# Keeping the lo parts of w_in and w_out in DRAM, and forming the down projection's right factors in other units

## The chip, the cores and the metric

The kernel runs on one core of a Trainium2 chip. The metric is device time in microseconds (us) of one execution, as the median of several. The engines are TensorE (PE in the profile; its weight loads are listed apart as PEld), VectorE (DVE), ScalarE (ACT), GpSimd (POOL) and SyncE (SP), which here only issues DMAs; 16 DMA engines move the data.

## What is computed

One layer of a hybrid decoder for 1024 prompt tokens and 64 sample tokens (8 sequences of 8), all in float32. Cut to what matters:

```python
x = x + 0.5 * rms_norm(swiglu(rms_norm(x, g1), w_gu1, w_down1), p1)     # first FFN
z = rms_norm(x, gm) @ w_in + b_in                                       # 1024 x 2816
q, k, v, hq, hf, hi, hg = split(z)
a = windowed attention with sinks (q, k, v)
o = chunkwise gated linear recurrence (hq, hf, hi)
x = x + rms_norm(concat(norm(a), norm(o) * silu(hg)) @ w_out, pm)       # 1024 x 1024
x = x + 0.5 * rms_norm(swiglu(rms_norm(x, g2), w_gu2, w_down2), p2)     # second FFN
```

## The kernel before

**Chunks.** The tokens are cut into three chunks: chunk 0 has 256 prompt tokens and the 64 sample tokens (width 320), chunks 1 and 2 have 384 prompt tokens each (`WIDTH`, L26). Weights are read anew from DRAM for each use; SBUF does not hold them.

**Hi and lo.** A float32 matrix product is made of three products of a reduced type (`mm3`, L276: lines L278, L279 and L280). Each operand is split into hi, a rounded copy made on ScalarE, and lo, the difference, made by a subtraction on VectorE (`split`, L256: L257 and L258). `load_w` (L260) loads a weight tile of 512 KB into one of three `raw` buffers on SP's queue, takes a hi and a lo buffer from a pool (`wsp`, 8 buffers, so four tiles) and calls `split`. Chunk 0, 1 and 2 each load and split the same tiles of w_in (22 tiles: 18 column tiles by `col_tile`, four row tiles for hi) and of w_out (8 tiles).

**The mixer.** `w_in_units(n)` makes z for chunk n, `mixer(n)` the attention and the recurrence, `w_out_units(n)` the projection back. The order is at the end of `tile_step`: w_in for chunk 0, then the rest of the first FFN's down projection beside the mixer of chunk 0, then w_in for chunk 1, w_out for chunk 0, w_in for chunk 2, and so on. Mixers run as generators: each `tick()` in the code around lets them go a step further, so that their many small matmuls come to stand between the large ones. Instructions of each engine are put in order when the program is built and run in that order.

**The FFN of chunks 1 and 2.** Both chunks are computed together in each FFN by a scheme with seven products in the place of eight (Strassen's). The up projection (`up`, L847) runs over 22 units. In unit u the steps are `product(u, m)` for m = 1, 2, 6, 5, 7 in turn, and m = 4 and 3 of a unit are placed inside the next one. `evict(u, m)` takes the results out of TensorE's banks, with one multiplication on GpSimd for m = 4 and one for m = 3 (L745). The down projection needs combinations of activations (left factors) and of the weights w_down (right factors):

- `left(u)` (L768) runs when an odd unit's m = 3 is evicted: four additions on GpSimd over two units' outputs and two stores to DRAM (`FA`).
- `right_load(u)` (L780) loads four half rows of w_down on SP into two of 12 `big` buffers; `right_form(u)` (L788) makes four additions on GpSimd (L791, L792, L795, L796), in the first FFN also two splits (`in_place`), and two stores to DRAM (`FB`).

In `up`, `d` (L852) says for which odd number a right factor is loaded at a unit's m = 1 and formed at its m = 7: number 1 in unit 2, number u in unit u for the odd u from 3 on.

**The down projection** reads activations (`act`, L876, and in `begin_pair`, L936) and weights back from DRAM through `raw` and other buffers.

Of the kernel before, what the change touches and what calls it, by code (L numbers as in the profile page):

```python
# [1 line left out]

# [6 lines left out]
F32 = mybir.dt.float32  # L9
F32R = mybir.dt.float32r  # L10
# [8 lines left out]
P = 128  # L19
# [25 lines left out]
def tile_step(ctx: ExitStack, tc: tile.TileContext, A: dict, O: list):  # L45
# [224 lines left out]
    def wsrc(w, c0, n=P):  # L270
        return w[:, c0:c0 + n].rearrange("(k p) m -> p k m", p=P)
# [375 lines left out]
    def make_ffn(wgu, wdn, h, tag):  # L647
# [199 lines left out]
        def up(hooks={}):  # L847
            for i, (kind, u, m) in enumerate(f.steps):
                if kind == "p" and m == 1 and u in hooks:
                    hooks[u]()  # L850
                if kind == "p":
                    d = 1 if u == 2 else u if u % 2 and u > 1 else 0  # L852
                    if m == 1 and d:
                        right_load(d)
                    product(u, m)
                    evict(u, m)
                    if m == 7 and d:
                        right_form(d)
# [58 lines left out]
        def begin_pair(ms, inner):  # L917
            def weight(m, ks):
                n, k0 = len(ks), ks[0]
                if m in halves:  # L920
                    hi, lo = [pp.tile([P, 2, 512], F32R, tag="wsp", bufs=8, name=uid("w")) for _ in range(2)]
                    nc.sync.dma_start(hi[:, :n].bitcast(F32), FH[:, k0:k0 + n, halves[m]])
                    nc.sync.dma_start(lo[:, :n].bitcast(F32), FB[:, k0:k0 + n, {7: 0, 4: 2}[m]])
                    return hi, lo
                raw = rawslot((P, 2, 512))
                if m in (1, 2, 3):
                    r, half = (k0 if m == 1 else k0 + NK), m == 3
                    nc.sync.dma_start(raw[:, :n], wdn[r * P:(r + n) * P, half * 512:half * 512 + 512].rearrange(
                        "(k p) m -> p k m", p=P))
                else:  # L930
                    nc.sync.dma_start(raw[:, :n], FB[:, k0:k0 + n, {7: 0, 5: 1, 4: 2, 6: 3}[m]])
                hi, lo = [pp.tile([P, 2, 512], F32R, tag="wsp", bufs=8, name=uid("w")) for _ in range(2)]
                split(hi[:, :n], lo[:, :n], raw[:, :n])
                return hi, lo

            def act(m, ks):  # L936
                n, k0 = len(ks), ks[0]
                t = hslot(1).rearrange("p (k l) w -> p k l w", k=2)
                if inner:
                    raw = f.pool.tile([P, 2, 384], F32, tag="wf", bufs=4, name=uid("ar"))  # L940
                else:
# [78 lines left out]
    def mixing(tp, h):  # L1020
# [14 lines left out]
                        channel_multiplier=0)  # L1035
        G.tensor_copy(own, of)
        Z, KX, VN, MT = {}, {}, {}, {}
        state = [None]

        def bias(c):  # L1040
            return cols[:, C_BIN + c:C_BIN + c + 1]

        def col_tile(c):
            if c < 4:
                return load_w([(slice(0, 64), wsrc(w_in, 64 * c, 64)),
                               (slice(64, 128), wsrc(w_in, 256 + 64 * c, 64))], pp, "wsp", 8)
            return load_up(w_in, c * P)

        def w_in_units(n):
            w = WIDTH[n]  # L1050
# [1 line left out]
            z = Z[n] = {}  # L1052

            def tr(c, dst):
                wt = col_tile(c)
                bank = mmbank()
                proj(bank[:, :w], wt, h[n], w, range(4))
                tick()
# [458 lines left out]
        return w_in_units, mixer, w_out_units  # L1517


    def seq(*gens):  # L1520
# [70 lines left out]
                                pre_s(n, y, g, part, f2.SF, x2N[n - 1])), RB1)  # L1591

    with tc.tile_pool(name="mx", bufs=1) as tp:
        w_in_units, mixer, w_out_units = mixing(tp, hmix)
        need("c0")
        w_in_units(0)
        stream("m0", mixer(0), RM[0])
# [121 lines left out]
```

## Time and profile before

| | |
|---|---|
| Median of 3 runs | 2006.6 us (2004.51 to 2008.71) |
| Profiled execution | 2007.94 us |
| Its span, first to last instruction | 2006.2 us |
| Granted TensorE clock | 0.999 |
| Largest groups | L278, L279 and L280, all shapes: TensorE |
| Moved by DMA | 370.31 MB, 185 GB/s over the span |

Up to about 100 us the first columns of the first FFN are computed for chunk 0 alone, to about 490 its up phase runs, to about 600 the down projection of chunk 0, from about 650 to 735 w_in for chunk 0, to 855 the rest of the first FFN's down projection with the mixer of chunk 0. The mixing part of chunks 1 and 2 goes to about 1400, the second FFN to the end, its up phase from about 1435 to 1740.

A row of the profile names a line of the kernel, an engine, an operation and the tiles as out<-in, with the count, the busy time, the mean of one in ns, and the idle time before with what ended it. A wait is put down to whatever came last by semaphore. A matmul's end is modelled, so that a busy TensorE need not be at its peak; how many matmuls start in a stretch tells more.

### The profile page before, as it was taken

What the parts mean: (1) busy time and instruction counts of PE and PEld (TensorE: products, weight loads), DVE (VectorE), ACT (ScalarE), POOL (GpSimd) and SP (SyncE); (2) the same over time, 40 slices, a digit from 0 to 9 for tenths busy, and PEclk for the clock granted to TensorE, in tenths of its full rate; (3) what the DMA queues carried; (4) which work ended last, traced back from release to release, by engine and by line L of the source; (5) the groups of instructions that cost most, each with busy time, mean ns of one, the idle gap of its engine ahead of it and who ended that gap; (6) DMA issues with size and microseconds to landing.
All of it is one profiled execution on the core that took longest, in us unless ns stands there. A gap on an engine that the chain in (4) does not pass through costs nothing.

```text
span 2006.2 us, 34709 instructions
## 1 busy us (share of the span) xinstructions
PE 1983.4 (99%) x13349; PEld 1856.0 (93%) x13349; DVE 1410.5 (70%) x2303; ACT 934.5 (47%) x1689; POOL 541.5 (27%) x508
## 2 busy tenths in 40 slices
PE   9999999999999999999999999999999999999998
PEld 8999999999998987798899898988999999999886
DVE  6676667887558655777667756857888878655666
ACT  7544333444455434435344544746544444444452
POOL 0013443655104101211212311220155565510201
PEclk9999999999999999999999999999999999999999
DMA  8545446566766756766434243527566555577874
GB/s 259 169 122 179 132 129 215 202 221 226 235 217 219 190 150 215 256 166 190 135 93 144 85 143 106 175 89 235 153 198 211 184 192 192 208 231 234 285 260 138
DMA packets 377319, 370.31 MB, mean 185 GB/s; under 512 B 40546, under 2 KB 294321, under 8 KB 377137
## 3 DMA queue, kind: packets, MB, share of 16 engines
q1 hardware_dynamic: 371169, 357.21, 56.2%
q10 hardware_dynamic: 5984, 10.88, 1.6%
q8 instruction: 105, 1.72, 0.4%
q14 instruction: 61, 0.50, 0.1%
HBM read 284.31 MB, written 84.71 MB: 184 GB/s over the span
## 4 chain that ended last, share of the span: by engine, by line
PE 87%; DVE 5%; DMA 5%; ACT 2%; issue 2%; SPq 0%; DVEq 0%; ACTq 0%
PE mm L278 26%; PE mm L280 25%; PE mm L279 25%; DMA raw<-in_ffn_w_gu_dram 2%; DMA ar<-act 2%; PE pv L1196 1%; PE c L278 1%; PE c L280 1%; PE c L279 1%; PE sc L1155 1%; DVE t L707 1%; DVE w L258 1%; PE pT L1183 1%; DVE wspl L258 1%; DMA ar<-fa 1%
## 5 line engine op out<-in xcount | busy, mean ns | idle before, releaser
L278 PE MATMUL mm<-h,wsph 128*128 128x320 f32 (+1 forms) x1296 | 412.1, 320 | 2.9 <-ACT wsph L257 1.3
L280 PE MATMUL mm<-h,wspl 128*128 128x320 f32 (+1 forms) x1296 | 409.1, 317 | 1.9 <-DVE wspl L258 1.8
L279 PE MATMUL mm<-h,wsph 128*128 128x320 f32 (+1 forms) x1296 | 409.6, 317 | 0.4 <-DVE h L258 0.4
L257 ACT CAST wsph<-raw 128x1024 fp32r<-128x1024 f32 x202 | 211.4, 1049 | 280.5 <-PE mm L279 211.9
L258 DVE TENSOR_TENSOR wspl<-raw,wsph 128x1024 fp32r<-128x1024 f32 x202 | 253.1, 1257 | 123.3 <-ACT wsph L257 120.7
L258 DVE TENSOR_TENSOR w<-raw,w 128x512 fp32r<-128x512 f32 (+1 forms) x214 | 223.9, 1050 | 87.4 <-ACT w L257 86.0
L257 ACT CAST w<-raw 128x512 fp32r<-128x512 f32 (+1 forms) x214 | 158.1, 742 | 216.1 <-PE mm L279 111.7
L278 PEld LDWEIGHTS mm<-h,wsph 128*128 128x128 f32 x1296 | 242.8, 188 | 7.4 <-issue 2.5
L280 PEld LDWEIGHTS mm<-h,wspl 128*128 128x128 f32 x1296 | 243.0, 188 | 5.8 <-DVE wspl L258 2.7
L279 PEld LDWEIGHTS mm<-h,wsph 128*128 128x128 f32 x1296 | 243.3, 188 | 2.4 <-issue 1.1
L278 PE MATMUL mm<-h,w 128*128 128x384 f32 x704 | 235.4, 335 | 1.5 <-DVE big L761 1.5
L279 PE MATMUL mm<-h,w 128*128 128x384 f32 x704 | 235.6, 335 | 0.0
L280 PE MATMUL mm<-h,w 128*128 128x384 f32 x704 | 230.2, 335 | 0.0
L278 PE MATMUL mm<-w,h 128*128 128x512 f32 x462 | 181.0, 395 | 1.1 <-DVE big L956 1.1
L745 POOL TENSOR_TENSOR big<-big 128x384 f32<-128x384 f32 x88 | 113.4, 1288 | 252.5 <-ACT big L758 143.8
L279 PE MATMUL mm<-w,h 128*128 128x512 f32 x462 | 181.1, 392 | 0.0
L280 PE MATMUL mm<-w,h 128*128 128x512 f32 x462 | 179.7, 391 | 0.0
L278 PE MATMUL mm<-big,w 128*128 128x384 f32 x528 | 176.8, 335 | 1.9 <-ACT big L748 1.1
L279 PE MATMUL mm<-big,w 128*128 128x384 f32 x528 | 176.5, 334 | 0.0
L280 PE MATMUL mm<-big,w 128*128 128x384 f32 x528 | 176.4, 334 | 0.0
L258 DVE TENSOR_TENSOR w<-t,w 128x512 fp32r<-128x512 f32 x176 | 160.7, 922 | 10.7 <-ACT w L257 10.3
L278 PEld LDWEIGHTS mm<-h,w 128*128 128x128 f32 x704 | 132.1, 188 | 1.8 <-DVE big L761 1.8
(358 smaller groups left out, 3854.6 us busy)
## 6 DMA issues: line engine op xcount, KB each, us to landing
raw<-in_ffn_w_gu_dram SPq DMA_DIRECT2D x156, 512.0 KB
raw<-in_ffn_w_down_dram SPq DMA_DIRECT2D x74, 512.0 KB
raw<-in_w_in_dram SPq DMA_DIRECT2D x54, 512.0 KB
ar<-fa SPq DMA_DIRECT2D x70, 384.0 KB
big<-in_ffn_w_down_dram SPq DMA_DIRECT2D x88, 256.0 KB
fb<-big SPq DMA_DIRECT2D x44, 512.0 KB
fa<-big SPq DMA_DIRECT2D x22, 768.0 KB
raw<-fb SPq DMA_DIRECT2D x30, 512.0 KB
```

The source lines that it names most:

```text
L257: S.copy(hi, src)
L258: (lo_eng or V).tensor_tensor(lo, src, hi.bitcast(F32), op=ALU.subtract)
L278: PE.matmul(out, a[0], b[0], start=first, stop=False, skip_group_check=resume)
L279: PE.matmul(out, a[0], b[1], start=False, stop=False, skip_group_check=resume)
L280: PE.matmul(out, a[1], b[0], start=False, stop=last, skip_group_check=resume)
L707: V.tensor_tensor(t, x, y, op=ALU.subtract)
L745: G.tensor_tensor(e[:, i], e[:, i], e[:, i + 1], op=ALU.mult)
L1155: PE.matmul(banks[g][:, i * 256:i * 256 + wk], zq[64 * g:64 * g + 64, 2 * pr + i, b * P:(b + 1) * P], kx[64 * g:64 * g + 64, k0:k0 + wk], ...
L1183: PE.transpose(bank[:, (i * nk + kb) * P:(i * nk + kb + 1) * P], pt[g][:, i, kb * P:(kb + 1) * P], ident)
L1196: PE.matmul(ob[:, hd * 64:hd * 64 + 64], pT[g][:, (i * nk + kb) * P:(i * nk + kb + 1) * P], vn[:, vb, g * 64:g * 64 + 64], start=kb == 0, ...
```

## The change

1. **Lo parts.** A new function `load_lo` takes the place of `load_w` for w_in and w_out. In chunk 0 it splits as before and also stores the lo part to new DRAM tensors (LI, LV, LO) from SP's queue. In chunks 1 and 2 the hi part is still cast from the loaded tile on ScalarE, but the lo part is loaded from DRAM by a DMA that ScalarE issues ahead of that cast; for w_out there are two such DMAs a tile, since chunk 0 works by columns and the others by rows. The first load of chunk 1's w_in is ordered behind the last activation load of the first FFN (`behind`).
2. **Right factors.** `d` is now number 1 in unit 2, number 3 in unit 3, and number u + 1 in unit u for the even u from 4 on.

```diff
-                    d = 1 if u == 2 else u if u % 2 and u > 1 else 0
+
+                    d = 3 if u == 3 else 1 if u == 2 else u + 1 if u % 2 == 0 and u > 2 else 0
...
-                nc.sync.dma_start(raw[:, :n], FA[:, k0:k0 + n, SLOT[m]])
+                f.last_load = nc.sync.dma_start(raw[:, :n], FA[:, k0:k0 + n, SLOT[m]]).ins
...
+        LI, LV, LO = [dr.tile([P, k, KC * P], F32, name=x) for k, x in ((22, "li"), (4, "lv_"), (KC, "lo"))]
+
+        def load_lo(n, src, at, shape=(P, KC, P), part=None):
+            raw = rawslot(shape)
+            for sl, ap in src:
+                with tc.issue_after(behind.pop()) if n and behind else nullcontext():
+                    nc.sync.dma_start(raw if sl is None else raw[:, :, sl], ap)
+            hi, lo = [pp.tile(list(shape), F32R, tag="wsp", bufs=8, name=uid("wsp" + x)) for x in "hl"]
+            if n == 0:
+                split(hi, lo, raw)
+                nc.sync.dma_start(at, lo.bitcast(F32))
+            else:
+                if part:
+                    hf, kk = part
+                    for k in range(2):
+                        nc.scalar.dma_start(lo[:, k].bitcast(F32).rearrange("p (d m) -> p d m", d=4),
+                                          LO[:, 4 * hf:4 * hf + 4, (2 * kk + k) * P:(2 * kk + k) * P + P])
+                else:
+                    nc.scalar.dma_start(lo.bitcast(F32), at)
+                S.copy(hi, raw)
+            return hi, lo
...
-                wt = load_w([(None, ap)], pp, "wsp", 8, (P, 2, 512))
+                wt = load_lo(n, [(None, ap)], LV[:, kk].rearrange("p (k m) -> p k m", k=2), (P, 2, 512))
...
-                    wt = load_up(w_out, d * P)
+                    wt = load_lo(n, [(None, wsrc(w_out, d * P))], LO[:, d].rearrange("p (k m) -> p k m", k=KC))
...
-                    wt = load_w([(None, ap)], pp, "wsp", 8, (P, 2, 512))
+                    wt = load_lo(n, [(None, ap)], None, (P, 2, 512), (hf, kk))
...
         need("c1")
+        behind.append(f1.last_load)
         w_in_units(1)
```

`col_tile` now takes the chunk's number and calls `load_lo` with the tile's place in LI. Numbers, shapes and order of the matmuls' accumulation stay.

More of the change, by code (lines that the diff above doesn't have):

```diff
@@ L1 @@
-from contextlib import ExitStack
+from contextlib import ExitStack, nullcontext
 import concourse.bass as bass
@@ L1037, in mixing @@
         Z, KX, VN, MT = {}, {}, {}, {}
+        behind = []
         state = [None]
@@ L1041, in bias, with col_tile @@
             return cols[:, C_BIN + c:C_BIN + c + 1]
-        def col_tile(c):
+        LI, LV, LO = [dr.tile([P, k, KC * P], F32, name=x) for k, x in ((22, "li"), (4, "lv_"), (KC, "lo"))]
[18 more added lines that the diff above has]
+            return hi, lo
+        def col_tile(n, c):
+            src = [(None, wsrc(w_in, c * P))]
             if c < 4:
-                return load_w([(slice(0, 64), wsrc(w_in, 64 * c, 64)),
-                               (slice(64, 128), wsrc(w_in, 256 + 64 * c, 64))], pp, "wsp", 8)
-            return load_up(w_in, c * P)
+                src = [(slice(0, 64), wsrc(w_in, 64 * c, 64)), (slice(64, 128), wsrc(w_in, 256 + 64 * c, 64))]
+            return load_lo(n, src, LI[:, c].rearrange("p (k m) -> p k m", k=KC))
         def w_in_units(n):
@@ L1054, in tr @@
             def tr(c, dst):
-                wt = col_tile(c)
+                wt = col_tile(n, c)
                 bank = mmbank()
@@ L1515, in w_out_units @@
                     V.tensor_tensor(y[hf][:, i], y[hf][:, i], g, op=ALU.mult)
-        return w_in_units, mixer, w_out_units
+        return w_in_units, mixer, w_out_units, behind
     def seq(*gens):
@@ L1593, in tile_step @@
     with tc.tile_pool(name="mx", bufs=1) as tp:
-        w_in_units, mixer, w_out_units = mixing(tp, hmix)
+        w_in_units, mixer, w_out_units, behind = mixing(tp, hmix)
         need("c0")
```

## The prediction

> **What bounds the kernel now.** I read the page first (span, busy times), then the table of 50 us stretches, then the list of what TensorE waited for.
>
> ```profile
> span 2006.2 us, 34709 instructions
> PE 1983.4 (99%) x13349; PEld 1856.0 (93%) x13349; DVE 1410.5 (70%) x2303; ACT 934.5 (47%) x1689; POOL 541.5 (27%) x508
> ```
>
> The profiled execution took 2007.94 us, 1.7 us more than its span; the median of the runs shown is 2006.6 us. TensorE is busy 99% of the span, so the question is how much of the rest can go.
>
> ```profile
> 350.00:400.00 50.00, 49.22 (x284) 48.90 (x284) 43.81 (x54) 23.50 (x47) 29.55 (x20) 1.00 0.60 209
> 450.00:500.00 50.00, 48.87 (x283) 48.55 (x282) 39.25 (x41) 22.76 (x41) 29.37 (x22) 1.00 0.62 218
> 500.00:550.00 50.00, 47.73 (x315) 46.94 (x314) 27.04 (x26) 21.93 (x30) 9.58 (x7) 1.00 0.73 243
> 750.00:800.00 50.00, 48.70 (x377) 39.12 (x376) 28.53 (x67) 24.30 (x60) 5.81 (x11) 1.00 0.68 215
> 800.00:850.00 50.00, 49.04 (x440) 38.75 (x439) 37.99 (x103) 22.12 (x55) 15.49 (x21) 1.00 0.75 254
> 1250.00:1300.00 50.00, 49.11 (x542) 46.20 (x541) 40.28 (x99) 32.39 (x64) 11.52 (x19) 1.00 0.56 173
> 1350.00:1400.00 50.00, 49.36 (x289) 44.70 (x288) 34.06 (x69) 30.93 (x62) 0.00 (x0) 1.00 0.72 221
> 1450.00:1500.00 50.00, 48.49 (x280) 48.07 (x279) 41.38 (x56) 22.14 (x44) 25.95 (x19) 1.00 0.63 205
> 1500.00:1550.00 50.00, 50.00 (x290) 50.00 (x289) 44.52 (x48) 21.17 (x41) 31.88 (x23) 1.00 0.61 206
> ```
>
> Columns: stretch, length, busy time and count of TensorE, weight loads, VectorE, ScalarE and GpSimd, granted clock, DMA share, GB/s. Away from both ends of the span these, less the full row of 1500 (one of many like it), are the stretches in which TensorE lacks most, and it lacks at most 2.3 us of 50. Where it lacks nothing the cadence is fixed: 290 matmuls in 50 us is 172 ns each.
>
> ```profile
> PE mm L278 <- DVE big L761: 2.1, 2, 1.5
> PE mm L280 <- DVE wspl L258: 1.8, 2, 1.3
> PE lv L1228 <- DVE big L1346: 1.1, 1, 1.1
> PE mm L278 <- ACT big L748: 1.1, 1, 1.1
> PE mm L278 <- DVE big L956: 1.1, 2, 0.9
> PE mm L278 <- ACT sg L668: 1.1, 2, 0.9
> PE mm L278 <- ACT big L753: 0.8, 1, 0.8
> PE mm L278 <- ACT wsph L257: 0.6, 1, 0.6
> PE mm L279 <- DVE h L258: 0.4, 1, 0.4
> ```
>
> These are TensorE's waits from 50 us on (the start is not touched): who waited for whom, us in total, times, longest. They add up to 10.1 us. **That is all the waiting that any edit in the middle could remove**, 0.5% of the time. No matmul is removed.
>
> **Right and left factors.** The change moves the loading and forming of the right factors from units 5, 7, ... 21 to 4, 6, ... 20; units 2 and 3 keep theirs. Count and size of GpSimd's adds, of SP's loads (four per pair) and of the stores stay; only their place moves. In the built order, GpSimd's queue for one pair of units was: two products, three right adds, a product, the fourth right add, one left add, a product, three left adds. All eight adds lay in one stretch. Afterwards it is right adds with a product among them, a product, one left add, a product, three left adds, a product. The last right factor is also done a unit earlier, so it no longer lies at the start of the down projection.
>
> What the bunching costs is seen in VectorE's rows before the wait of 0.8 us in the stretch of 350:
>
> ```profile
> 338.38 0.68 DVE L258 TENSOR_TENSOR w<-raw,w 128x512 fp32r<-128x512 f32 x1
> ...
> 339.61 1.39 POOL L745 TENSOR_TENSOR big<-big 128x384 f32<-128x384 f32 x1 [1.70 <-DVE big L761]
> ...
> 340.05 1.50 DVE L258 TENSOR_TENSOR w<-raw,w 128x512 fp32r<-128x512 f32 x1
> ```
>
> One operation on one shape takes 0.68 us while GpSimd is idle (it was, for the 1.70 us before 339.61) and 1.50 us beside its adds. VectorE's instructions run in order, so a run of eight adds delays it by up to 8 x 0.8 = 6.6 us; behind it wait the evictions that free TensorE's banks. Spread out, the total delay is the same but each burst is about half, and the next product's 2.1 us (12 x 172 ns) absorbs more of it. I count what hangs on it: 0.8 (ACT L753, stretch of 350) and 1.1 (ACT L748, stretch of 450) in the first up phase, recovered by three quarters, -1.4; 2.3 at the start of the first down projection (stretch of 500: h L258, one of L761, one of wspl), where one right factor's casts, subtractions and stores leave the queues, recovered by two fifths, -0.9; 0.5 (the other wspl) at the second down projection, -0.2. The 1.5 us (L761) in the stretch of 1450, where the second up phase begins, stays, since units 2 and 3 are unmoved. **Sum -2.5; bounds -4.7 (all of these) and +2**, were the new order to make two waits like the ones it removes.
>
> **Lo parts.** Chunk 0 splits as before and adds 30 stores of 512 KB on SP (22 for w_in, 8 for w_out). Chunks 1 and 2 drop 60 subtractions on VectorE and add 76 DMA issues on ScalarE's queue (44 of 512 KB, 32 of 256 KB).
>
> ```profile
> L258 DVE TENSOR_TENSOR wspl<-raw,wsph 128x1024 fp32r<-128x1024 f32 x202 | 253.1, 1257 | 123.3 <-ACT wsph L257 120.7
> ```
>
> ```profile
> 706.56 0.34 ACTq L405 DMA_DIRECT2D gb<-in_norm_ffn_post_dram  x1
> 706.89 1.28 ACT L1097 ACT_TABLE_LOAD   x1
> ```
>
> ```profile
> 850.00:1000.00 150.00, 150.00 (x1158) 131.67 (x1157) 108.53 (x232) 68.51 (x129) 23.65 (x31) 1.00 0.59 164
> 1000.00:1150.00 150.00, 150.00 (x1346) 137.31 (x1345) 109.53 (x270) 67.31 (x147) 40.79 (x60) 1.00 0.38 108
> ```
>
> VectorE loses 60 x 1.257 = 75 us of work, ScalarE gains 76 x 0.34 = 26 us and one more table load of 1.28 us. But in 850 to 1150, where 44 of the 60 lie, TensorE is busy 300 of 300 us: the subtractions were hidden, and removing them buys nothing there. What the relief can reach is 1.1 (L1346), 1.1 (L956), 1.1 (sg) and 0.6 (the second wsph): 3.9 us. The first two lie ahead of chunk 1's w_in and the last two end in ScalarE, which gets more work; I take -1.5.
>
> Against it stands the lo's arrival. ScalarE's cast already waits until TensorE frees the buffer, so the added issue waits for the same event. Behind it on ScalarE stand that cast, the mixer's exponentials and the copies out of TensorE's banks, as they stood behind the cast, now 0.34 us later; TensorE waits for those copies. The lo then comes by DMA:
>
> ```profile
> 744.76 4.12 DMA ar<-fa
> ```
>
> ```profile
> L280 PEld LDWEIGHTS mm<-h,wspl x323: 186/188/192, 855.9 to 1129.5; 128*128 128x128 f32 x162
> ...
> L258 DVE TENSOR_TENSOR wspl<-raw,wsph x52: 1204/1224/2127, 848.8 to 1128.7; 128x1024 fp32r<-128x1024 f32 x52
> ```
>
> The first row, of the chain of waits, is a read back of 384 KB; the others tell when wspl is read by weight loads and when it is written (first and last start). By it 512 KB land 4.12 x 4/3 = 5.5 us (estimate) after an issue of 0.34 us, where the subtraction took 1.2: the lo is ready 4.6 us later. The first lo of chunk 1 was ready at 850.0 and used at 855.9, 5.9 us ahead; later tiles come every 5.5 us (280 us / 51) with four pairs of buffers, so they are further ahead. Only the first tile of a run can be late, worst where a run starts without lead, as before the 0.6 us wait for wsph in 1350 to 1400. Bounds 0 and +5; I take +1, since three of the runs follow other tiles of the same pool.
>
> The stores of chunk 0 are the dearest unknown:
>
> ```profile
> 650.00:660.00 10.00, 10.00 (x55) 8.91 (x55) 7.60 (x10) 6.32 (x10) 0.00 (x0) 1.00 1.14 257
> 660.00:670.00 10.00, 10.00 (x71) 9.99 (x71) 6.83 (x9) 5.36 (x10) 1.32 (x2) 1.00 0.95 257
> 680.00:690.00 10.00, 10.00 (x70) 10.00 (x69) 4.80 (x6) 3.15 (x3) 0.00 (x0) 1.00 0.53 156
> ```
>
> ```profile
> L280 PEld LDWEIGHTS mm<-h,wspl x144: 187/188/188, 656.3 to 736.0; 128*128 128x128 f32 x144
> ...
> L258 DVE TENSOR_TENSOR wspl<-raw,wsph x22: 1209/1226/1417, 648.8 to 723.3; 128x1024 fp32r<-128x1024 f32 x22
> ```
>
> A 0.524 MB store occupies the engines for 0.524e6 / 257e3 x 1.14 = 2.3 us by the row of 650, or 0.524e6 / 243e3 x 0.73 = 1.6 us by the row of 500, whose transfers have longer runs; the store has 4 KB a partition, so I take 1.6. On SP each store waits for the subtraction that also frees the raw buffer of the load right behind it, so the wait is not new; the load starts one issue and one store later. Tiles come every 3.5 us (74.5 us / 21): 0.53 + 1.6 / 3.5 = 0.99 of the DMA engines. It just fits, and the splits lead TensorE by 656.3 - 650.0 = 6.3 us at the first tile and about 8 at the last (736.0 less a tile's 3.5, against 724.5). Covered, so 0; without cover it is the second rival below. The eight stores for w_out lie in 850 to 1150, a tile every 5.5 us: at most 0.59 + 1.6 / 5.5 = 0.88, so 0. The first load of chunk 1's w_in now has to follow the last load of the pair before it; that load stood behind it on SP before, so nothing queues longer but that first tile, whose lead is the 5.9 us above.
>
> The lo reads of chunks 1 and 2 take 44 x 1.6 us in those 300 us, 0.23 on top of 0.59 and 0.38: at most 0.82, so 0.
>
> By the Trainium skill, "DMA: Bandwidth & Descriptors", section "Issuing engines are not separate DMA queues", transfers issued by ScalarE run on the same 16 engines as SP's; that speaks against the change, since with a path of their own the lo reads would add nothing to those shares. No run here shows two queues sharing yet; by the one the sum has 0 and a smaller margin, by the other 0.
>
> **Sum:** -2.5 - 1.5 + 1.0 + 0 = **-3.0 us**; 2007.94 - 3.0 = 2004.9 for the profiled execution, 2006.6 - 3.0 = **2003.6 us** on the median. About 0.2%, 4 us, is what a measurement of this kernel can tell from no change, so the forecast lies inside that. Its own range is 2001 (five of the 10.1 us gone, and a little for the spread of the runs) to 2006.
>
> **The rivals.** (1) *More of the waits go.* Both parts recover nearly all they can reach, 4.7 + 3.9 = 8.6, less 2 for new waits: -6.5, 2000.1 us. For it: five of the nine rows, 6.5 of 10.1 us, name VectorE, which gets 75 us less. Against: stretches without waits are already at VectorE 44.5 of 50 (row of 1500), so backlog is not the only cause.
>
> (2) *The stores clog chunk 0's w_in; slower.* Place: 650 to 700. Six splits fall into the crowded 20 us (one in 3.5 us), so six stores of 2.3 us want 14 us where the share is already 1.14 and 0.95, and after that 0.53 + 2.3 / 3.5 = 1.19 stays above 1, losing 0.66 us a tile for 16 tiles, 10 us. Of 24 us the lead covers 6 to 8: up to +16; I take half, +8, 2014.6 us. It decides once a store costs more than (1 - 0.53) x 3.5 = 1.65 us. For it: the row of 650. Against: the loads there are cut into short runs, the stores are not.
>
> (3) *Late starts.* The lo by DMA and ScalarE's extra 26 us make two or three starts of w_in and w_out late: +4, 2010.6 us, where ScalarE already is what ends the waits. Against: the leads above.
>
> (4) *The idle time understates the room.* TensorE's waits under the profile's resolution shrink with VectorE's load. The busy share of weight loads in 850 to 1150 is 269 of 300, so 31 us: 1975 us. Against: the two rows hold 2504 matmuls, many of them small, and no wait. The Trainium skill, "Perfetto Trace Analysis", section "Identifying the Most-Contended Engine", calls matmul busy time a poor measure of headroom and weight-load busy a good one; by that rule this rival would be likelier, but the fixed cadence of 172 ns speaks against it here.
>
> **How the numbers follow.** Forecast 0.45 (0.36 of it inside 0.2%, 0.09 faster); rival 1 0.25 (faster); rival 4 0.02 (faster); rival 2 0.18 (slower); rival 3 0.10 (0.06 slower, 0.04 inside). So faster 0.36, same 0.40, slower 0.24. The range runs from 1998.5 (all but 2 us of what can go, leaving out rival 4 and the best of rival 1, 0.08) to 2012 (all of rival 3, leaving out the upper two thirds of rival 2, 0.12).
>
> **What would show it.** Right: TensorE's lack in the stretches of 350, 450 and 500 gone or halved, that of 1450 still there; VectorE's subtractions into wspl 142 instead of 202; no wait of TensorE between 650 and 740. Wrong: TensorE's loss in 600 to 750 above 1 us with the DMA share near 1 throughout (rival 2); waits for wspl ended by a DMA in 850 to 1400 (rival 3); matmul cadence changed where nothing waited (rival 4); or a new row of more than 1.5 us in the list of TensorE's waits in an up phase, which would say that the new order of GpSimd's adds is no better.

## The result, and the profile after

| | before | after |
|---|---|---|
| Median (22 runs each) | 2007.4 us | 2010.3 us |
| Ratio after / before, 95% interval | | 1.0015 (1.0009 to 1.0021) |
| Span of the profiled execution | 2006.2 us | 2009.9 us |
| TensorE's waits of 0.1 us and more, from 50 us on | 10.1 us | 13.4 us |

The changed kernel is 3 us slower: 0.0015 of 2007.4, between 1.8 and 4.2. The forecast was 3 us faster. That is inside the 0.2% which the prediction took as the limit of what can be told, but with 22 runs each it is clear of no change, and on the other side.

From the page after:

```profile
PE 1983.7 (99%) x13349; PEld 1855.8 (92%) x13349; DVE 1335.5 (66%) x2243; ACT 935.6 (47%) x1690; POOL 523.6 (26%) x508
```

VectorE lost the 75 us of subtractions that the prediction counted (1410.5 to 1335.5), and TensorE gained nothing from it. The stretches after, with the columns of the prediction's table:

```profile
350.00:400.00 50.00, 49.55 (x286) 49.06 (x285) 38.16 (x50) 22.44 (x44) 26.29 (x21) 1.00 0.59 190
400.00:450.00 50.00, 48.86 (x280) 48.22 (x279) 40.88 (x50) 21.48 (x42) 27.53 (x21) 1.00 0.61 203
450.00:500.00 50.00, 48.96 (x283) 48.64 (x282) 35.03 (x43) 23.09 (x43) 24.55 (x19) 1.00 0.65 215
500.00:550.00 50.00, 48.66 (x323) 48.29 (x322) 26.24 (x25) 22.39 (x31) 9.68 (x7) 1.00 0.74 241
...
800.00:850.00 50.00, 48.88 (x432) 38.70 (x431) 34.84 (x95) 21.58 (x61) 13.39 (x20) 1.00 0.88 292
850.00:900.00 50.00, 48.55 (x363) 44.78 (x362) 28.32 (x86) 22.50 (x49) 4.21 (x8) 1.00 0.85 242
1050.00:1100.00 50.00, 48.50 (x462) 45.42 (x463) 30.98 (x92) 20.45 (x37) 14.21 (x23) 1.00 0.75 228
1350.00:1400.00 50.00, 48.40 (x276) 43.28 (x275) 27.63 (x62) 27.82 (x57) 0.00 (x0) 1.00 0.84 246
1450.00:1500.00 50.00, 48.63 (x280) 48.21 (x279) 41.25 (x52) 22.33 (x44) 30.57 (x22) 1.00 0.72 229
```

The lack at 500 is down from 2.3 to 1.3 us. The lacks at 350 and 450 (0.8 and 1.1) have become three from 350 to 500 (0.5, 1.1 and 1.0). New lacks stand at 850 and 1050, where TensorE was full before, and that of 1350 has grown from 0.6 to 1.6. And whom TensorE waited for, after:

```profile
PE mm L278 <- ACT big L755: 2.6, 4, 1.0
PE mm L278 <- ACT wsph L1065: 1.8, 2, 1.1
PE mm L280 <- DVE wspl L258: 1.5, 2, 1.3
PE lv L1253 <- POOL t L1289: 1.5, 1, 1.5
PE mm L278 <- DVE big L761: 1.4, 1, 1.4
PE mm L278 <- ACT sg L668: 1.1, 2, 0.9
PE lv L1253 <- DVE big L1371: 1.0, 1, 1.0
PE oT L1156 <- DVE t L1152: 0.8, 1, 0.8
PE pv L1221 <- DVE t L1211: 0.7, 1, 0.7
PE mm L279 <- DMA wspl<-lo: 0.5, 1, 0.5
PE lv L1253 <- DVE t L1287: 0.4, 1, 0.4
```

(Behind L853 the lines are those of the changed kernel: L1065 is the hi cast in `load_lo`, L1371 is L1346 of before, L1253 L1228, L1289 L1264.) Six rows are new: L755 four times in the first up phase, oT, pv and, on VectorE at 821, lv in chunk 0's mixer, lv on GpSimd at 1082 in chunk 1's, and the lo itself once, at chunk 2's w_out at 1361.

One more view is needed for what follows. All kernels have 13,349 recorded TensorE matmuls, so the start of the n-th one can be compared. This table, worked out from the traces, gives how much later than before the n-th matmul starts, in us, with the difference at number 300 (the first loads, which vary by a us either way) taken off. In places the order of the matmuls differs; at the numbers chosen both kernels stand at the same work. The columns e1 to e14 are the experiments below.

```
number  before  after     e1     e3     e9    e13     e5    e14    e10
  3000   495.1   +1.4   +1.8   +0.5   -0.3   +0.5   +0.6   +0.2   +0.5
  3300   543.8   +0.0   +0.5   +0.9   -0.3   -0.1   +0.9   +0.4   -0.1
  4800   779.8   -0.1   +0.2   +0.4   -0.7   -0.1   +0.7   +0.4   -0.3
  6600  1007.1   +2.7   -0.4   -1.0   +1.6   +2.5   +2.6   +9.3   -1.0
  7800  1146.8   +1.8   -0.4   -1.0   +1.6   +2.5   +2.6   +9.3   -3.5
  9300  1312.5   +1.8   -0.4   -1.0   +1.7   +2.6   +2.6   +9.4   -3.5
  9900  1385.9   +2.7   -0.4   -1.0   +1.6   +2.5   +2.6   +9.3   -2.7
 13348  1997.4   +2.7   -1.0   -0.6   +0.8   +2.6   +2.8  +10.2   -3.5
```

After: +1.4 in the first up phase and as much back at the start of the down projection; level with before at 780; **+2.8 from 780 to 1007**; 0.9 won by 1147; 0.9 lost again at chunk 2's w_out. The second feed-forward changes nothing. Each column is one execution: at number 3000 the kernels with the old order of the right factors lie between -0.4 and +1.2, so +1.4 there is hardly outside what they show among themselves.

### The profile page after: what moved, and what is told of

It is laid out like the page before. It is cut to its first block, busy times and chain, and to the rows that moved or that the text cites. A ratio compares the mean times of both kernels' runs of the same rounds, so it can differ in the third digit from the quotient of the medians.

```text
span 2009.9 us, 34735 instructions
## 1 busy us (share of the span) xinstructions
PE 1983.7 (99%) x13349; PEld 1855.8 (92%) x13349; DVE 1335.5 (66%) x2243; ACT 935.6 (47%) x1690; POOL 523.6 (26%) x508
## 4 chain that ended last, share of the span: by engine, by line
PE 75%; DMA 10%; DVE 8%; ACT 3%; issue 2%; POOL 1%; SPq 1%; ACTq 0%; DVEq 0%; POOLq 0%
PE mm L278 22%; PE mm L280 22%; PE mm L279 22%; DMA raw<-in_ffn_w_gu_dram 4%; DVE t L707 2%; DVE w L258 2%; DMA ar<-fa 2%; DMA big<-in_ffn_w_down_dram 1%; DMA ar<-act 1%; PE c L278 1%; PE c L280 1%; PE c L279 1%; PE pv L1221 1%; PE sc L1180 1%; DMA big<-in_x_prompt_dram 1%
## 5 line engine op out<-in xcount | busy, mean ns | idle before, releaser
L258 DVE TENSOR_TENSOR w<-raw,w 128x512 fp32r<-128x512 f32 (+1 forms) x214 | 213.3, 1001 | 82.0 <-ACT w L257 80.5
L258 DVE TENSOR_TENSOR wspl<-raw,wsph 128x1024 fp32r<-128x1024 f32 x142 | 179.5, 1267 | 117.1 <-ACT wsph L257 110.8
L257 ACT CAST wsph<-raw 128x1024 fp32r<-128x1024 f32 x142 | 148.7, 1049 | 192.1 <-PE mm L279 103.3
L745 POOL TENSOR_TENSOR big<-big 128x384 f32<-128x384 f32 x88 | 109.0, 1238 | 290.1 <-ACT big L758 200.7
L258 DVE TENSOR_TENSOR w<-t,w 128x512 fp32r<-128x512 f32 x176 | 165.2, 948 | 16.8 <-ACT w L257 16.6
```

The lines of the kernel that those rows point to most:

```text
L257: S.copy(hi, src)
L258: (lo_eng or V).tensor_tensor(lo, src, hi.bitcast(F32), op=ALU.subtract)
L745: G.tensor_tensor(e[:, i], e[:, i], e[:, i + 1], op=ALU.mult)
```

## The experiments

Theory A was, after this reading: the lo reads cost the time, by late first tiles and a new order of the mixer's work. Its rivals were B (the new order of the right factors) and C (chunk 0's stores). All ratios are to the kernel before on the same chip, with 95% intervals; 0.001 is 2.0 us.

| run | what differs from before | ratio | interval |
|---|---|---|---|
| e1 | right factors only | 1.0000 | 0.9992 to 1.0009 |
| e2 | lo parts only | 1.0014 | 1.0006 to 1.0023 |
| e3 | chunk 0's stores only | 1.0009 | 1.0000 to 1.0018 |
| e4 | lo parts, no order rule | 1.0026 | 1.0017 to 1.0035 |
| e5 | lo parts, read in chunk 1 only | 1.0027 | 1.0017 to 1.0036 |
| e6 | lo parts, read in chunk 2 only | 1.0025 | 1.0015 to 1.0035 |
| e7 | lo parts, reads issued by SP | 1.0037 | 1.0025 to 1.0049 |
| e8 | right factors, casts on VectorE | 1.0015 | 1.0006 to 1.0023 |
| e9 | order rule only | 1.0014 | 1.0005 to 1.0022 |
| e10 | stores, read in chunk 2, no rule | 1.0001 | 0.9993 to 1.0010 |
| e11 | stores twice | 1.0103 | 1.0087 to 1.0118 |
| e12 | right factors where they paid | 0.9991 | 0.9982 to 1.0000 |
| e13 | stores and order rule | 1.0019 | 1.0010 to 1.0028 |
| e14 | stores, read in chunk 1, no rule | 1.0037 | 1.0025 to 1.0049 |
| e15 | chunk 1 stores, chunk 2 reads w_in | 1.0008 | 0.9999 to 1.0017 |
| e16 | e15 and e12 together | 0.9997 | 0.9988 to 1.0005 |

### e1: the right factors alone

The kernel before with the new line for `d`.

> The kernel before with only the new order of the right factors. Theory A (the lo reads cost the time): -0.6 us against the kernel before (2.6 us of waits in the first up phase instead of 1.9, 0.9 less at the start of the first down projection, 0.4 less in the second feed-forward). Theory B (the new order of the right factors costs the time): +3 us or more, with new waits of TensorE beyond the four on the bank copies of product 7 in the first up phase.

1.0000. B falls: the right factors are not what made the kernel slower. They are no gain either: +1.8 us by number 3000 in this trace, 1.3 of it won back by 3300. Theory A's -0.6 lies inside the interval (-1.6 to +1.8 us). In the trace the four waits on L755 are there (3.0 us), the waits at the start of the down projection are 1.4 instead of 2.3, and those from 800 to 870 and on the lo at 1361 are absent.

### e2: the lo parts alone

The changed kernel with the old line for `d`.

> The changed kernel with the old order of the right factors, so only the lo parts in DRAM. Theory A: +3 to +4 us, the waits of TensorE between 750 and 860, at 1080 and at 1360 present (about 4 us more than before), those on product 7's bank copies absent. Theory B: within 1 us of before. Theory C (stores): +3, but lost between 600 and 750.

1.0014, +2.8 us (1.2 to 4.6): about the whole loss is in this part. The waits stand where A put them, but for the one at 1082, which is absent here, and in all they are 2.2 us more than before, not 4.

### e3: the stores alone

```diff
-                if part:
...
-                S.copy(hi, raw)
+                split(hi, lo, raw)
...
-        behind.append(f1.last_load)
```

> As the run before it, but chunks 1 and 2 form their lo on VectorE as the kernel before does and read nothing back; chunk 0 still stores its 30 lo tiles, and the order against the last load of the pair stays. Theory A: within 0.5 us of the kernel before. Theory C (the stores cost the time): +3 us, with TensorE's lack in 600 to 750 over 1 us larger.

The kernel differs from its expectation in one point: the order rule had been taken out as well (e13 puts it back). 1.0009, from 0 to 3.6 us. Its profile shows no loss at all: TensorE has no wait between 540 and 740, and its waits add up to 8.9 us. Theory C's loss in 600 to 750 isn't there; whether the stores cost a us elsewhere isn't told by this run.

### e4: no order rule

```diff
-        behind.append(f1.last_load)
```

> The lo parts alone, without the rule that chunk 1's first w_in load follows the last load of the pair before it. If that rule makes chunk 1's first tile late (the wait of 0.7 us on wsph at 863), the time falls by 0.7 us against the run with the rule and that wait is gone; if the lateness comes from ScalarE's queue, both stay as they are.

The other way: 1.0026, more than with the rule. The wait on wsph at 863 is gone, as the first case said, but in its place stand waits on the sample attention's loads (1.2 us on the cache at 860) and on ScalarE. The rule protects something; the question became what it costs.

### e5 and e6: one chunk's reads at a time

`if n == 0` becomes `if n != 1` for the split in e5, `if n != 2` in e6; the rule stays in both.

> The lo parts alone, but only chunk 1 reads them back; chunk 2 forms them on VectorE as the kernel before does. Theory A (each stretch in which reads replace subtractions pays for its own late start and its own new order): TensorE's waits between 815 and 870 stay at about 3.2 us, those near 1360 go back to 0.6; in all +2.4 us against the kernel before. Theory D (the traffic of the reads is what costs, and both chunks read 30 tiles): +1.5 us, spread over 850 to 1130, with no waits of their own.

> The lo parts alone, but only chunk 2 reads them back. Theory A: waits between 815 and 870 at most 0.9 us as before, those near 1360 at 1.5 instead of 0.6; in all +0.8 us against the kernel before. Theory D: +1.5 us, as chunk 1 alone.

Both 1.0025 or more, against both theories. In e6 chunk 1 reads nothing, and yet TensorE waits 4.7 us between 740 and 870 (2.2 before), in another order of the mixer than before; the profiled execution of e6 was the longest of its ten (2016.95 us, median 2011.54), so the size is not to be relied on, but the order is that of the program. So chunk 1's reads cannot be what moves chunk 0's mixer. Counting, of the 252 instructions of VectorE between 700 and 870, those that follow another instruction than before gave the next theory: 65 to 68 in the five kernels so far with the order rule (after, e2, e5, e6, e7), 0, 5 and 0 in e1, e3 and e8 without it, and 25 in e4, where chunk 1 reads without it. Not explained: e5 and e6 each cost more (+5.4 and +5.0 us) than e2, which has the reads of both chunks (+2.8); the intervals overlap.

### e7: the reads issued by SP

```diff
-                    nc.scalar.dma_start(lo.bitcast(F32), at)
+                    nc.sync.dma_start(lo.bitcast(F32), at)
```

(Both places of the call.)

> The lo parts alone, with the reads issued by SP instead of ScalarE. If ScalarE's 76 issues are what makes the casts and the lo late, the waits at 864 (0.7) and 1360 (1.5) go and the time falls by 1.5 us against the lo parts alone. If the order is what costs, whoever issues, the time stays within 1 us of theirs; if SP's queue, where the reads now stand ahead of the loads, is the tighter one, it rises by 2 us or more with waits on raw loads.

1.0037, 4.6 us more than e2. The third case holds in part: the wait on the lo at chunk 2's w_out grew to 0.6 and 2.5 us, but on the lo, not on raw loads. ScalarE's issues were not the cost.

### e8: the kept factors' casts on VectorE

e1, with these lines for `split` in `in_place`:

```diff
-                split(hi, t.bitcast(F32R), t)
+                V.tensor_copy(hi, t)
+                V.tensor_tensor(t.bitcast(F32R), t, hi.bitcast(F32), op=ALU.subtract)
```

> The new order of the right factors alone, with the hi casts of the two kept right factors on VectorE instead of ScalarE. If product 7's bank copies are late because those casts stand before them in ScalarE's queue and wait for GpSimd, the four waits of the first up phase (3.0 us) fall under 0.5 us and the time is 2 us under that of the new order alone. If the copies are late for the bunched adds themselves, the four waits stay above 2 us.

The four waits on L755 are gone, so those casts did hold product 7's copies up. But the time is 1.0015, and another copy waits instead. TensorE's waits of e8 from 300 to 540:

```profile
PE mm L278 <- ACT big L753: 4.2, 3, 2.0
```

L753 is product 6's copy. At the longest of the three (2.0 us at 428) it stands behind an activation that waits 1.8 us for VectorE's L750, and VectorE had waited 3.1 us for a weight load ahead of that. So taking the casts away from ScalarE cured the place and not the time; whether they delay those loads wasn't tried.

### e9: the order rule alone

```diff
+    behind = []
...
+            with tc.issue_after(behind.pop()) if behind else nullcontext():
+                nc.sync.dma_start(raw if sl is None else raw[:, :, sl], ap)
-            nc.sync.dma_start(raw if sl is None else raw[:, :, sl], ap)
...
-                nc.sync.dma_start(raw[:, :n], FA[:, k0:k0 + n, SLOT[m]])
+                f.last_load = nc.sync.dma_start(raw[:, :n], FA[:, k0:k0 + n, SLOT[m]]).ins
...
         need("c1")
+        behind.append(f1.last_load)
```

> The kernel before with one thing of the change: chunk 1's first w_in load has to follow the pair's last load on SP. No lo is stored or read. In the runs so far every kernel with this rule has a new order of the mixer's instructions between 740 and 870 and waits there, and every kernel without it has the old order. Theory F (the rule, not the reads, makes chunk 0's mixer late): +1.7 us, TensorE's waits between 815 and 870 about 2.5 instead of 0.9, and the lv matmuls late by VectorE there. Theory A (the reads make it late): within 0.5 us of the kernel before, with its order.

**1.0014, +2.8 us: this one rule of the change costs about as much as all of it**, with no lo stored or read; Theory A's "within 0.5 us" is outside the interval (1.0 to 4.4). 60 of VectorE's 252 instructions follow another than before. What the rule does is seen on SP's queue, before first, then e9 (DMA issues; L943 and L946 are the activation loads, L264 and L267 load chunk 1's first tiles of w_in):

```profile
850.00 1.01 SPq L264 DMA_DIRECT2D raw<-in_w_in_dram  x2
851.06 0.78 SPq L943 DMA_DIRECT2D ar<-fa  x1
```

```profile
838.77 0.42 SPq L946 DMA_DIRECT2D ar<-fa  x1
840.47 1.75 SPq L267 DMA_DIRECT2D raw<-in_w_in_dram  x2
```

Before, the last activation load stood behind two of chunk 1's loads. With the rule it stands ahead of them, and the whole of the pair's work around it was put in another order when the program was built. Where the waits come from is seen on VectorE, before and then e9. L1262 and L1186 (L1265 and L1189 in e9) make what the mixer's lv and pv matmuls read; L258 splits an activation of the pair; L441 adds x at the end of a norm, and L399 (L402) begins the nine small instructions of the next:

```profile
817.77 0.41 DVE L1262 TENSOR_TENSOR t<-t,big 128x256 f32<-128x256 f32 x1
...
819.76 0.95 DVE L258 TENSOR_TENSOR h<-ar,h 128x768 fp32r<-128x768 f32 x1
...
836.01 0.68 DVE L1186 COPY t<-pT 128x512 f32<-128x512 f32 x1
836.94 0.31 DVE L399 SCALAR_TENSOR_TENSOR sm<-sm 128x3 f32<-128x3 f32 x1 [0.25 <-ACT junk L393]
```

```profile
815.98 0.96 DVE L258 TENSOR_TENSOR h<-ar,h 128x768 fp32r<-128x768 f32 x1 [2.63 <-ACT h L257]
...
819.52 0.42 DVE L1265 TENSOR_TENSOR t<-t,big 128x256 f32<-128x256 f32 x1
...
833.03 1.24 DVE L441 SCALAR_TENSOR_TENSOR big<-big,sm,xt 128x512 f32<-128x512 f32 x1 [0.56 <-DMA xt<-in_x_prompt_dram]
835.12 0.16 DVE L402 SCALAR_TENSOR_TENSOR sm<-sm 128x3 f32<-128x3 f32 x1 [0.85 <-ACT junk L396]
...
838.10 0.68 DVE L1189 COPY t<-pT 128x512 f32<-128x512 f32 x1
```

Before, the mixer's two instructions run ahead of the split and of the norm. In e9 they stand behind them, and the split waits for its cast (2.63), the norms for a load (0.56) and for ScalarE (0.85), while the engine does nothing else. TensorE's rows for it in e9, the first at 820, the second at 839:

```profile
PE lv L1231 <- DVE t L1265: 1.0, 1, 1.0
...
PE pv L1199 <- DVE t L1189: 0.7, 1, 0.7
```

These waits are not the whole. Between numbers 4800 and 6600 the profiled execution of e9 loses 2.3 us to before, and TensorE's waits there (1.9 us against 0.9) are 1.0 of it. Another 1.0 is lost where TensorE shows no wait, in the matmuls that update the state of the sample tokens' recurrence (su, 32 rows each). Before, four of them stand together; in e9 the same four stand in two pairs (the first line is before, the other two e9):

```profile
964.17 1.13 PE L1435 MATMUL su<-t,t 32*128 32x512 f32 x4
```

```profile
968.64 1.12 PE L1438 MATMUL su<-t,t 32*128 32x512 f32 x2
...
970.69 1.12 PE L1438 MATMUL su<-t,t 32*128 32x512 f32 x2
```

Two take as long as four: in the group of four the first two start 7 ns apart and so do the last two, while in the pairs the second starts 0.5 us behind the first. The remaining 0.3 us isn't placed. One limit: this execution of e9 was the shortest of its eleven (2008.36 us, median 2010.92), and where an ordinary one loses more wasn't recorded.

### e10: chunk 2's reads without the rule

e6 without its line `behind.append(f1.last_load)`.

> Chunk 0 stores its lo, only chunk 2 reads them back, and the rule for chunk 1's first load is left out. Theory F: the mixer of chunk 0 keeps its old order and the waits between 740 and 870 are at most those of before (2.2); left is the late lo at chunk 2's w_out near 1360, +0.9 us; 3 us less than the same kernel with the rule. Theory A: as with the rule, +3 us or more.

1.0001 instead of e6's 1.0025, and the mixer of chunk 0 is all but back in its old order (5 of 252 follow another instruction) with waits of 1.3 us there. The late lo at chunk 2's w_out is there too (0.8). Not foreseen: between 1007 and 1147 e10 wins 2.6 us, where TensorE shows no wait in either kernel. Before, then e10:

```profile
1035.00:1150.00 115.00, 115.00 (x1036) 103.92 (x1036) 89.79 (x227) 52.03 (x114) 35.47 (x51) 1.00 0.38 112
```

```profile
1035.00:1150.00 115.00, 115.00 (x1055) 105.23 (x1054) 73.14 (x214) 55.24 (x114) 30.96 (x51) 1.00 0.63 189
```

Both are busy for 115 of 115 us, but 1055 matmuls start instead of 1036. Most of it is in how the mixer's small matmuls stand. The score matmuls (sc, 64 rows each) come in groups of eight or of four, and a group of either size takes as long, as two lines of the kernel before show:

```profile
1065.96 1.13 PE L1155 MATMUL sc<-kx,big 64*128 64x256 f32 x8
...
1098.53 1.13 PE L1155 MATMUL sc<-kx,big 64*128 64x256 f32 x4
```

In the group of eight, every second one starts 7 ns behind the one before it; in the group of four each starts 0.2 us or more behind. From 1007 to 1147 before has one group of eight and six of four; e10 has three of eight and two of four, two groups fewer, which is 2.1 of the 2.6 us. Between numbers 6600 and 7800 all seven experiments in which chunk 2 reads its lo (e2, e4, e6, e7, e10, e15, e16) win 2.6 us, and all nine others nothing. The reads also raise the DMA share there from 0.38 to 0.63.

### e11: every store twice

```diff
-                nc.sync.dma_start(at, lo.bitcast(F32))
+                for x in at:
+                    nc.sync.dma_start(x, lo.bitcast(F32))
```

(e3 with a second set of DRAM tensors.)

> Chunk 0 writes each of its 30 lo tiles twice, to two places; nothing is read back and no order rule is set. If the stores are free, the time stays within 1 us of the kernel before and TensorE has no wait between 540 and 740. If a store costs what the run with one store each hinted at (+1.7 us in the mean for 30), it is +3.4 us; if the DMA engines are full (1.0 of them by 3.5 us a tile with one store), chunk 0's w_in loses 5 us or more in 600 to 750.

1.0103, +21 us. Chunk 0's w_in in the kernel after, with one store a tile, and then in e11:

```profile
660.00:680.00 20.00, 20.00 (x140) 19.99 (x138) 11.37 (x14) 7.24 (x12) 1.25 (x2) 1.00 0.99 299
680.00:700.00 20.00, 20.00 (x139) 20.00 (x138) 11.25 (x16) 8.75 (x8) 2.67 (x4) 1.00 0.97 328
700.00:720.00 20.00, 20.00 (x105) 16.65 (x104) 11.77 (x15) 9.27 (x9) 1.69 (x4) 1.00 1.00 335
```

```profile
660.00:680.00 20.00, 18.12 (x123) 17.58 (x121) 8.00 (x12) 5.40 (x9) 1.31 (x2) 1.00 1.06 333
680.00:700.00 20.00, 17.19 (x101) 16.40 (x102) 8.91 (x10) 6.66 (x7) 0.00 (x0) 0.91 0.99 344
700.00:720.00 20.00, 17.84 (x104) 16.76 (x103) 10.16 (x14) 8.47 (x9) 3.65 (x7) 0.91 1.06 401
```

With one store the DMA engines are full and TensorE lacks nothing; with two it lacks 7 us in these 60. By the starts of its matmuls e11 is 10.3 us behind before at number 4800 and 16.8 at 5400 (860 us); what costs the second part wasn't traced. The prediction's second rival lay one store away.

### e12: the right factors where they paid

In the first feed-forward only the last pair moves (number 21 in unit 20); the second has the new line for `d`.

> The kernel before with the new order of the right factors only where it paid in the trace: the last pair of the first feed-forward and all of the second. If the parts add up: the waits of 340 to 480 as before (0.8), those of 480 to 540 about 2.0 instead of 3.4, the second feed-forward 0.3 less; -1.5 us against the kernel before. If the gain at the start of the down projection came from the whole new order, 0.

0.9991, from -3.6 us to 0; the expected -1.5 lies inside. The parts came otherwise than expected: TensorE's waits from 340 to 480 are 1.8 us instead of 0.8, those from 480 to 540 1.3 instead of 3.4. Its median is the lowest of all sixteen (2006.0), and its interval just touches no change.

### e13 and e14: the stores with the rule, chunk 1's reads without it

e13 is e3 with the rule; e14 is e5 without it.

> Chunk 0's 30 stores and the order rule for chunk 1's first load together; nothing is read back (the run with the stores alone had no rule, other than its expectation says). If the rule is the cause and the stores add the 1.7 us of their own run: +3 to +4.5 us. If only the rule counts: +2.9 us as the rule alone. If only the stores count: +1.7 us.

> Only chunk 1 reads its lo back, without the order rule. By the times at equal matmul numbers, the reads of chunk 1 without the rule cost 6 us between 820 and 940 (two waits of about 1 us in the sample attention among them): +6 us against the kernel before, and nothing after 1000. If those 6 us came from chunk 2's reads in the same program, 0 to +1.

e13: 1.0019, 3.8 us, in the range of the first case. Beside e9 (1.0014) the stores add 1 us, as they may add 1.8 in e3; each interval alone reaches to nothing or nearly so. e14: 1.0037, +7.4 us, the first case in size (+6): reads of chunk 1 are what makes the rule needful. TensorE's waits in e14 from 800 to 960 begin

```profile
PE skT L1370 <- DMA kv<-in_cache_k_win_dram: 1.3, 1, 1.3
PE spv L1408 <- DMA kv<-in_cache_v_win_dram: 0.9, 1, 0.9
```

so the sample attention's loads come late when chunk 1's loads and reads start as early as they can. This execution was the longest of five (2018.0 us, median 2015.03), and the rest of the 9.3 us at number 6600 isn't traced.

### e15 and e16: a version that might beat both

e15 has no rule, stores the 22 lo tiles of w_in in chunk 1 and reads them in chunk 2; w_out is split in all chunks. e16 adds e12.

> No rule; chunk 1, not chunk 0, stores the 22 lo tiles of w_in and chunk 2 reads them; w_out is split as before. If the stores of chunk 0 cost something in their crowded place and chunk 2's reads save the 2.6 us that their trace shows between 1035 and 1147: -2.5 us against the kernel before, no wait near 1356 on a lo. If the 2.6 us came with the reads of w_out or with luck in the order: 0 to -1.

> The same with the new order of the right factors where it paid (last pair of the first feed-forward, all of the second). If the two gains add up: -2.5 - 1.9 = -4.4 us against the kernel before, which would beat both kernels.

e15's profiled execution is 2.9 us below before in span (2003.3), with 2.6 us won between 1007 and 1147 as in e10, but its twelve runs spread from 2005.06 to 2015.87 and give 1.0008. e16 gives 0.9997 (-2.4 to +1.0 us). The two gains did not add up to anything that the runs can tell; -4.4 is outside. e12 alone stays the better.

## Why the prediction was wrong

**The step that failed** is the last sentence on the stores: "The first load of chunk 1's w_in now has to follow the last load of the pair before it; that load stood behind it on SP before, so nothing queues longer but that first tile". The order on SP was seen rightly and priced at 0; e9, which has this rule alone, measures +2.8 us (1.0 to 4.4). Beside other parts it costs as well: e13 less e3 is +2.0, e6 less e10 +4.8, and between numbers 4800 and 6600 the seven kernels with the rule (after, e2, e5, e6, e7, e9, e13) lose 1.9 to 8.6 us to before, while the seven without it in which chunk 1 reads nothing and chunk 0 stores at most once lie between -1.4 and +0.7. The step looked at what queues behind that load on SP. It did not ask what a new edge does to the order in which every engine's instructions are laid out, an order that is fixed when the program is built. In the profile of e9, 1.0 of the 2.3 us lost are waits for VectorE, where work that TensorE needs now stands behind work that waits itself, and 1.0 is a group of small matmuls that fell apart. In the kernel after, 1.6 of its 2.8 us are added waits (0.7 of them on chunk 1's first hi cast); that group stays whole there, and where the other 1.2 us go is open. Nor could the rule simply be left out: with chunk 1's reads in the program, the kernel without it is slower still (e4 by 2.4 us beside e2, e14 by 2.0 beside e5).

**Right factors, forecast -2.5, measured 0** (-1.6 to +1.8). Two of the three terms were right: -0.9 at the start of the down projection (waits of 2.3 us there became 1.3), -0.2 at the second down projection (0.5 became 0.2), and the 1.5 us at 1464 stayed (1.4). The first up phase was forecast at -1.4 and is +1.4 (after) and +1.8 (e1) by the starts of the matmuls, so this is the term that failed: what the prediction kept for its bound of +2, new waits like the old ones, is what happened. The two old waits went nearly as said (0.2 us is left in e1); four new ones came, 2.6 us in the kernel after and 3.0 in e1. They are read on ScalarE and GpSimd of the changed kernel:

```profile
472.67 0.62 ACT L257 CAST fh<-big 128x512 fp32r<-128x512 f32 x1 [4.80 <-POOL big L792]
...
477.05 0.62 ACT L257 CAST fh<-big 128x512 fp32r<-128x512 f32 x1 [3.24 <-POOL big L796]
477.58 0.47 ACT L755 COPY big<-mm 128x384 f32<-128x384 f32 x1
```

```profile
469.12 1.29 POOL L791 TENSOR_TENSOR big<-big 128x512 f32<-128x512 f32 x1 [2.66 <-DMA big<-in_ffn_w_down_dram]
...
475.28 1.74 POOL L796 TENSOR_TENSOR big<-big 128x512 f32<-128x512 f32 x1
```

In the first feed-forward each pair's two kept factors are cast to hi on ScalarE (`in_place`). The right adds now come first in GpSimd's queue, and wait for their load; ScalarE waits 4.8 and 3.2 us for two of them, in order, and product 7's bank copy L755 stands behind. The prediction followed GpSimd's adds to VectorE, but not the two casts a pair that hang on them. The second feed-forward has no such casts, and no such waits.

**The relief of VectorE, forecast -1.5, measured nothing where it was looked for.** The wait on L1346 (1.1) is 1.0, that on sg 1.1 as before, that on wsph grew from 0.6 to 1.1. The two on L956 (1.1) are gone, but they are 0.2 or less in e1 and e3 too, where VectorE is relieved of nothing. What changed instead lies where the prediction saw no room, since it took the waits for "all the waiting that any edit in the middle could remove" and the cadence between them for fixed: with chunk 2's reads, 2.6 us are won from 1007 to 1147 without a wait in either kernel (e10). Rival 4 had the place right, "the idle time understates the room", with 2.6 us of it, not 31; its mechanism, waits too short to be seen, is not what the trace shows, since 2.1 us are groups of score matmuls that came together. In the kernel after, 1.5 us of that is lost again to the wait on GpSimd at 1082.

**The late lo, forecast +1.0 (0 to +5), inside its bounds:** 1.7 us of waits more, at the first tiles of chunk 1's w_in (0.7 on its hi cast) and of chunk 2's w_out (1.6 instead of 0.6, a third of it on the lo). **The stores, forecast 0,** cost nothing in their place; the share reached 1.00 against the 0.99 worked out. Over all they may cost 1 to 2 us (e3, and e13 beside e9), which the runs don't settle.

**Summed in runs:** order rule and stores +3.8 (e13), chunk 1's reads under the rule +1.6 (e5 less e13), chunk 2's reads -1.6 (e10 less e3), right factors 0: +3.8, where the change measured +3.0 (1.8 to 4.2). Terms 2 and 3 are differences of overlapping intervals, and the parts do not simply add: with chunk 2's reads taken under the rule (e6 less e13, +1.2) the sum would be +6.6. So the rule is shown to cost time by itself; the division of the whole +3.0 is not shown.

**The rivals.** Rival 3 came near the size (+4, 2010.6) and part of the place, late starts of w_in and w_out; the runs show its mechanism for 1.7 us of waits, not for the whole, so its number is partly luck. Rival 2 was false at one store and true at two. Rival 4's sign, a changed cadence of the matmuls where nothing waited, did appear, by another mechanism than its own.

## What to carry to other kernels

An edge that only orders two DMAs can have a price of its own, since the whole program may be laid out anew around it: run it alone, without what it was made for, and compare each engine's built order before pricing it at nothing. When additions are moved on one engine, follow each result to the engine that takes it next and to what stands behind that taker in its queue. Here TensorE was busy 99% of the time and hid 75 us of another engine's work, and taking that work away bought nothing by itself; the order of the instructions decided, on VectorE by who waits ahead of whom, on TensorE by whether small matmuls stand in one group or two.

## What the runs showed of the hardware

**The granted clock can fall behind short waits.** In e2 TensorE waits 0.8 and 0.6 us at 839 and 841, and then:

```profile
830.00:840.00 10.00, 8.81 (x107) 7.01 (x105) 6.71 (x19) 4.10 (x12) 3.67 (x4) 1.00 0.99 357
840.00:850.00 10.00, 9.43 (x47) 7.45 (x46) 5.91 (x17) 2.67 (x7) 2.07 (x5) 0.66 1.07 289
```

A clock of 0.66 over 10 us is up to 3.4 us, more than both waits, and e2 falls 3.6 us behind between numbers 5100 and 5400, of which its waits are 0.8 more than those of before. Over whole executions it shows too: the five of e6 with a mean clock of 0.997 took 2014.4 us in the mean, the four with 0.999 2009.9. The cost of the rule is not of this kind alone: the eight executions of e9 with 0.999 took 2010.2 us in the mean, the 17 of before beside them 2008.2. By the Trainium skill, "TensorE: Matmul & The Clock Gate", section "HAM oscillation — how this bites in real kernels", it takes idle gaps of more than about 3.4 us to lower the clock; this trace does not agree. The wait of 1.5 us at 1464 in the kernel before has no fall behind it, so a wait alone does not do it, and what else it takes is open.

**ScalarE's queue draws on the same DMA engines as SP's.** The prediction named the Trainium skill's "DMA: Bandwidth & Descriptors", section "Issuing engines are not separate DMA queues", with no run to show it. The rows of 1035 to 1150 now agree with it: with chunk 2's reads, issued by ScalarE, the share of the 16 engines goes from 0.38 to 0.63.

**A busy TensorE can still be 2% quicker.** The 115 us without a wait that e10 shortened by 2.6 us held the same matmuls in another order. Small matmuls that stand together started two at a time here: eight score matmuls of 64 rows take 1.13 us, as four do, and four updates of 32 rows take 1.13 us where two take 1.12. The busy time shows none of this.
